# A fifth buffer for the two weight parts, paid with four spare tiles, in a one-core decoder of four layers

## The chip, the core and the metric

The kernel runs on one core of a Trainium2 chip. The metric is the device time in microseconds (us) of one execution, as the median of several runs. The engines are TensorE (PE in the profile; PEld is its weight loading), VectorE (DVE), ScalarE (ACT), GpSimd (POOL) and SyncE (SP, whose queue issues most DMAs).

## The reference

A sequence of 1024 tokens of width 1024, all in float32, passes through a retention layer, a latent-attention (MLA) layer, a gated linear attention layer (GLA) and a feed-forward block. Cut to one layer, and to the form that the others share:

```python
h = rmsnorm(x, g_pre)
proj = h @ w_in                      # 1024 x 1024 @ 1024 x 6144 in the first layer
q, k, v, gate = jnp.split(proj, [...], axis=-1)
...                                  # rope, scores in chunks, running state, group norm
y = (jax.nn.silu(gate) * o) @ w_out
return x + rmsnorm(y, g_post)
```

The last block is two large GEMMs, the first feed-forward GEMM with its activation and the second one back to width 1024.

## The kernel before

**Products.** A float32 operand is split into a high part, cast to the fp32r type, and a low part, the rest: x = hi + lo, w = wh + wl. Each GEMM is three fp32r matmuls that sum in one accumulator: hi with wh (L230), lo with wh (L231), hi with wl (L232), in `mm3`. In `turned_product` (L524 to L526) the activations are the stationary operand and the weights the moving one; a product of 512 columns then comes as two halves of 256. Large GEMMs are made block by block with seven products in place of eight, so weights are needed in sums as well: the raw parts `ws` and `wsc` are loaded, `wsb` and further sums are made on GpSimd (`w_op`, L641).

**Weight parts.** `w_split` makes them from a raw tile: ScalarE copies to `wh` (L632), then VectorE subtracts to get `wl` (L633). `load_parts` does the same for plain weights (L143, L144). All pairs of the kernel come from two rings, `wh` and `wl`, of [128, 1024] tiles (4 KB in a partition), given out in turn. A pair can be written once PE has read the one that stood in its place.

**Jobs and stages.** Stage A (to 510 us) makes the inputs of the retention layer: jobs for q and k, V jobs (turned, seven pairs each) and gate jobs, four of each kind. From 510 to 800 come the retention itself and its output GEMM, then the input of stage B (800 to 1010, with `load_parts`), the attention and its output (to 1390). Stage C (1390 to 1740) makes the inputs of the GLA layer. Into its jobs a side chain is woven, `c_side` and `c_levels`: for each of 8 passes SyncE loads a log-decay `b`, ScalarE makes `qe` and `kd` of it, VectorE multiplies `kd` and `z`, and PE turns `kd` (L1786) and multiplies the levels (`ps_lv`, L1766). The GLA layer's cores and its output follow, to 1960. The first feed-forward GEMM runs to 2234, the second to the end.

**Tiles of the second feed-forward GEMM.** Its operands live in a list of free [128, 512] tiles (2 KB in a partition), `Slots`: `get` takes the first that is free, `put` appends. It works in groups, `FF2_GROUPS = (3, 3, 3, 3, 2, 2)`: a group of three loads `lo<-u` (21 tiles, each split at once into a high and a low part, so 42 tiles) and holds 28 tiles of sums. `F_SLOTS` adds spare tiles to the list:

```python
slots.add(fslots, [f"f{i}" for i in range(F_SLOTS)])
```

**Order.** Each engine works off its own queue in order, and the queues are written when the program is built: a scheduler with a timeline of its own places an instruction once its operands and buffers are free there, weights with high priority. Loads go through SyncE's queue (L122; weights L689). Stores go through ScalarE's queue (L119) in the stages A and B and through SyncE's after that. The number of buffers therefore decides not only how early a pair may be written on the chip, but where each split, load and store stands in its queue.

Of the kernel before, what the change touches and what calls it, by code (L numbers as in the profile page):

```python
# [14 lines left out]
F32R = mybir.dt.float32r  # L15
# [7 lines left out]
P = 128  # L23
# [15 lines left out]
C_WIDE = 2  # L39
C_WAIT = 16  # L40
C_LAST = 3
F_SLOTS = 7
C_TAIL = "01 11 21- 02 A 12 22- w0 w1 A 06 B 07 A 05 B w0 w2 04 A 03 B 16 17 B w1 15 14 13 w2 26- 27- 25- a 24- a 23- b"
C_NORM = "NP"
C_DVE = 3
# [36 lines left out]
def tile_kernel(ctx, tc, a, out):  # L82
# [3 lines left out]
    def pool(stack, name, bufs=1, space=None, side=None):  # L86
        kw = {}
        if space is not None:
            kw["space"] = space
        if side is not None:  # L90
            kw["side"] = side
        return stack.enter_context(
            tc.tile_pool(name=name, bufs=bufs, reuse_waits="tile", **kw)
        )

    cp = pool(ctx, "const")
    wp = pool(ctx, "weights")
# [26 lines left out]
    def load_w(*args, **kw):  # L124
        with tc.high_priority():
            return load_parts(*args, **kw)

    def load_parts(src, scale=None, nk=None):

        c = src.shape[-1]  # L130
        ws = wp.tile([P, 1024], F32, tag="ws", name="ws", bufs=2)[:, :c]
        nc.sync.dma_start(out=ws, in_=src)
        if scale is not None:
            w3 = ws.rearrange("p (k f) -> p k f", k=nk)
            nc.gpsimd.tensor_tensor(
                out=w3,
                in0=w3,
                in1=scale.unsqueeze(2).to_broadcast([P, nk, c // nk]),
                op=ALU.mult,
            )  # L140
        wh = wp.tile([P, 1024], F32R, tag="wh", name="wh", bufs=4)[:, :c]
        wl = wp.tile([P, 1024], F32R, tag="wl", name="wl", bufs=4)[:, :c]
        nc.scalar.activation(out=wh, in_=ws, func=AF.Copy)  # L143
        nc.vector.tensor_tensor(out=wl, in0=ws, in1=wh.bitcast(F32), op=ALU.subtract)  # L144
        return wh, wl
# [9 lines left out]
    def stage(name):  # L155
        return sp.tile([P, HALF], F32, tag="stage", name=name, bufs=4)
# [469 lines left out]
            self.direct(ps, (0, 1))  # L626

    def w_pair():
        return [wp.tile([P, 1024], F32R, tag=t, name=t, bufs=4) for t in ("wh", "wl")]

    def w_split(hi, lo, raw, lo_eng=nc.vector):
        nc.scalar.activation(out=hi, in_=raw, func=AF.Copy)  # L632
# [2 lines left out]
    def w_parts(raw, lo_eng=nc.vector):  # L635
        hi, lo = (t[:, : raw.shape[-1]] for t in w_pair())
        w_split(hi, lo, raw, lo_eng)
        return hi, lo
# [4 lines left out]
    def load_w7(src, pl):  # L643

        q = lambda t, i, n=1: t[:, i * 256 : (i + n) * 256]
        with tc.high_priority():
            ra = wp.tile([P, 1024], F32, tag="ws", name="ws", bufs=2)
            rb = pl.tile([P, HALF], F32, tag="ws7", name="ws7", bufs=1)
            nc.sync.dma_start(out=ra, in_=src)
            b12, b11, b21, b22 = (q(ra, i) for i in range(4))  # L650
            ha, hb = w_pair(), w_pair()

            def into(pair, c, n, src):
                w_split(*(q(t, c, n) for t in pair), src)

            into(ha, 0, 2, q(ra, 0, 2))
            w_op(q(rb, 0), b21, b22, ALU.add)
            w_op(q(rb, 1), b11, q(rb, 0), ALU.subtract)
            into(hb, 0, 2, rb)
            w_op(b21, b21, b11, ALU.subtract)  # L660
            into(ha, 2, 2, q(ra, 2, 2))
            w_op(b12, b12, q(rb, 1), ALU.add)
            into(hb, 2, 1, b12)
        w = {n: (q(ha[0], i), q(ha[1], i)) for i, n in enumerate((2, 1, 7, 4))}
        w.update({n: (q(hb[0], i), q(hb[1], i)) for i, n in enumerate((5, 6, 3))})
        return w

    class W7:
# [10 lines left out]
        def pair(self):  # L679
            return [t[:, : 2 * self.c] for t in w_pair()]  # L680
# [114 lines left out]
    with ExitStack() as ph:  # L795
# [87 lines left out]
        def job_of(n, early=False):  # L883
            product, src, f, i = jobs[n]
            w = W7(src, ap, 2 if product is turned_product else 1)
            if early:
                w.first()
            get = early_get if early else slots.get
            p = on_bank(product, bank5) if early else product
            return w, Fresh(p, get, lambda m, h, ts: f(i, m, h, ts))  # L890
# [17 lines left out]
        for n in range(len(jobs)):  # L908
            last = n == len(jobs) - 1
            drop = x7.drop if last else None  # L910
            if begun:
                w, c = begun.pop(0)
                c.product = jobs[n][0]
                w.rest(n >= 2)
            else:
                w, c = job_of(n)
# [652 lines left out]
    t = stage("mask")[:, : 7 * 64]  # L1569
# [296 lines left out]
    def job_of_c(n, early=False, bank=bank5):  # L1866
        product, src, f, i = c_jobs[n]
        w = W7(src, w7p, 2 if product is turned_product else 1)
        if early:
            w.first()  # L1870
        get = early_get_c if early and n < C_BEGIN else slots.get
        done = lambda m, h, ts: f(i, m, h, ts)
        return w, Fresh(on_bank(product, bank), get, done)
# [23 lines left out]
    for n in range(C_WIDE, len(c_jobs) - C_LAST):  # L1897
        if begun:
            w, c = begun.pop(0)
            w.rest(eng=nc.vector if n < C_DVE else nc.gpsimd)  # L1900
        else:
            w, c = job_of_c(n)
# [130 lines left out]
    for step in C_TAIL.split():  # L2033
# [4 lines left out]
        else:  # L2038
            w, c = last[int(step[0])]
# [51 lines left out]
    fslots = pool(ctx, "f_slots")  # L2091
    slots.add(fslots, [f"f{i}" for i in range(F_SLOTS)])

# [35 lines left out]
    def ff1_job(i, early=False):  # L2129
        w = W7(a["w_ff1"][i], w7p)  # L2130
        if early:
            w.first()
        done = lambda m, h, ts: u_done(i, m, h, ts)
        return w, Fresh(plain_product, slots.get, done)
# [4 lines left out]
    for i in range(16):  # L2139
        drop = x7.drop if i == 15 else None  # L2140
        if begun:
            w, c = begun.pop(0)
            w.rest()
        else:
            w, c = ff1_job(i)
# [283 lines left out]
```

## Time and profile before

| what | before |
| --- | --- |
| runs, us | 2575.43, 2577.38, 2582.12; median 2577.38 |
| profiled execution, us | 2580.32 |
| its span, first to last instruction, us | 2578.5 |
| granted clock of PE, mean | 0.977 |
| busy of the span: PE, DVE, ACT, POOL | 95%, 77%, 44%, 44% |

All rows below are of the profiled execution. Its time holds 1.8 us outside the span, and it lies 2.9 us above the median of the runs. A granted clock of 1.00 is the full 2.4 GHz, the level below it half of that. Names in the rows leave buffer numbers out (`wl` is any tile of that ring); [1.07 <-DVE wl L633] behind a row means that its engine was idle so long before it, and what ended that.

### The profile page before, as it was taken

The numbers are of one execution on the slowest core, as the hardware profiler recorded it, in microseconds if no ns is written. First come the engines' busy times: TensorE is split into PE (matmuls) and PEld (weight loads), VectorE is DVE, ScalarE is ACT, GpSimd is POOL, SyncE is SP. The second block draws the span as 40 slices with busy tenths as digits, with TensorE's granted clock in tenths as the row PEclk, the third lists the DMA queues.
The fourth block names the chain that finished last, engine by engine and source line by source line (L and its number), as shares of the span: only waits on it lengthen the run. The fifth ranks groups of instructions, "written<-read, shape, count | busy, mean of one in ns | idle before, by whom it ended". The sixth has DMA issues, their size and how long they took to land. (4 is left out here: it accounts for less than half of the span.)

```text
span 2578.5 us, 35600 instructions
## 1 busy us (share of the span) xinstructions
PE 2457.3 (95%) x12676; PEld 2058.8 (80%) x12676; DVE 1978.9 (77%) x2948; ACT 1130.4 (44%) x2033; POOL 1122.5 (44%) x834
## 2 busy tenths in 40 slices
PE   7999999999998999999999999989999999999998
PEld 5888888878776788888888788877777888788877
DVE  8787786789998863777659867787888777867886
ACT  7323323254443333555545365564453333543334
POOL 4354453534754521322203244444546666433355
PEclk8999999999998999999999999999999999999999
DMA  6423323533342222122234233456424444644432
GB/s 229 159 86 116 109 78 119 199 116 126 108 137 80 90 99 75 55 63 77 83 121 151 92 127 112 151 172 208 139 90 156 150 151 151 236 141 138 143 131 90
DMA packets 152670, 326.05 MB, mean 126 GB/s; under 512 B 17419, under 2 KB 20875, under 8 KB 152492
## 3 DMA queue, kind: packets, MB, share of 16 engines
q1 hardware_dynamic: 130604, 283.92, 33.4%
q10 hardware_dynamic: 21888, 39.86, 4.1%
q8 instruction: 100, 1.64, 0.3%
q14 instruction: 78, 0.64, 0.1%
HBM read 222.52 MB, written 99.09 MB: 125 GB/s over the span
## 5 line engine op out<-in xcount | busy, mean ns | idle before, releaser
L633 DVE TENSOR_TENSOR wl<-ws,wh 128x1024 fp32r<-128x1024 f32 (+3 forms) x200 | 211.2, 1063 | 24.7 <-ACT wh L632 23.7
L632 ACT ACTIVATE wh<-ws 128x1024 fp32r<-128x1024 f32 (+3 forms) x200 | 142.7, 725 | 198.3 <-PE ps L231 104.2
L641 POOL TENSOR_TENSOR wsb<-wsc 128x512 f32<-128x512 f32 (+2 forms) x72 | 101.4, 1409 | 252.7 <-issue 168.9
L230 PE MATMUL ps<-hi,wh 128*128 128x512 f32 (+1 forms) x488 | 185.8, 381 | 2.2 <-DVE y L2188 1.4
L232 PE MATMUL ps<-hi,wl 128*128 128x512 f32 (+1 forms) x488 | 183.9, 381 | 3.5 <-DVE wl L633 2.6
L231 PE MATMUL ps<-lo,wh 128*128 128x512 f32 (+1 forms) x488 | 185.4, 380 | 0.0
L632 ACT ACTIVATE wh<-wsb 128x1024 fp32r<-128x1024 f32 (+2 forms) x76 | 73.6, 968 | 222.6 <-PE ps L231 162.7
L641 POOL TENSOR_TENSOR ws<-ws,wsb 128x512 f32<-128x512 f32 (+2 forms) x72 | 102.1, 1418 | 122.2 <-DVE wl L633 104.7
L1430 POOL TENSOR_SCALAR p<-p,rl 128x512 f32<-128x512 f32 (+2 forms) x96 | 61.8, 655 | 191.7 <-DVE rl L1428 96.6
L641 POOL TENSOR_TENSOR wsb<-ws,wsb 128x512 f32<-128x512 f32 (+2 forms) x72 | 115.6, 1606 | 64.3 <-DMA ws<-w_a 41.1
L553 DVE TENSOR_TENSOR y<-ps,y 128x512 f32<-128x512 f32 x112 | 76.8, 686 | 72.2 <-PE ps L232 45.1
L553 DVE TENSOR_TENSOR y<-ps,one 128x512 f32<-128x512 f32 x108 | 73.7, 686 | 71.6 <-PE ps L232 27.8
L553 DVE TENSOR_TENSOR one<-ps,one 128x512 f32<-128x512 f32 x168 | 114.1, 682 | 12.7 <-PE ps L232 11.6
L633 DVE TENSOR_TENSOR wl<-wsc,wh 128x1024 fp32r<-128x1024 f32 (+2 forms) x76 | 109.5, 1445 | 8.6 <-ACT wh L632 8.1
L633 DVE TENSOR_TENSOR wl<-wsb,wh 128x1024 fp32r<-128x1024 f32 (+2 forms) x76 | 98.7, 1299 | 18.4 <-ACT wh L632 17.8
L232 PEld LDWEIGHTS ps<-hi,wl 128*128 128x128 f32 x488 | 91.7, 188 | 25.0 <-DVE wl L633 4.5
L641 POOL TENSOR_TENSOR wsc<-wsc,ws 128x512 f32<-128x512 f32 (+2 forms) x72 | 110.7, 1538 | 0.0
L230 PEld LDWEIGHTS ps<-hi,wh 128*128 128x128 f32 x488 | 91.7, 188 | 22.3 <-DVE y L2188 1.8
L231 PEld LDWEIGHTS ps<-lo,wh 128*128 128x128 f32 x488 | 91.7, 188 | 18.8
L2188 DVE TENSOR_TENSOR y<-ps,y 128x512 f32<-128x512 f32 x124 | 83.4, 683 | 29.6 <-PE ps L232 29.2
L632 ACT ACTIVATE wh<-wsc 128x1024 fp32r<-128x1024 f32 (+2 forms) x76 | 73.2, 969 | 59.3 <-PE ps L231 39.3
L188 DVE TENSOR_TENSOR lo<-lo,hi 128x512 fp32r<-128x512 f32 x106 | 77.5, 762 | 26.0 <-ACT hi L187 24.0
(468 smaller groups left out, 8543.5 us busy)
## 6 DMA issues: line engine op xcount, KB each, us to landing
lo<-u SPq DMA_DIRECT2D x98, 256.0 KB, 5.2
ws<-w_ff SPq DMA_DIRECT2D x23, 512.0 KB, 3.9
ws<-w_a SPq DMA_DIRECT2D x21, 512.0 KB, 4.7
u<-y SPq DMA_DIRECT2D x42, 256.0 KB, 2.1
ws<-w_b SPq DMA_DIRECT2D x17, 512.0 KB, 3.5
wsc<-w_a SPq DMA_DIRECT2D x16, 512.0 KB, 4.5
v<-v SPq DMA_DIRECT2D x32, 256.0 KB, 3.3
gate<-g SPq DMA_DIRECT2D x32, 256.0 KB, 3.4
```

The source lines that it names most:

```text
L188: (lo_eng or nc.vector).tensor_tensor(out=lo, in0=src, in1=hi.bitcast(F32), op=ALU.subtract)
L230: nc.tensor.matmul(ps, lh, rh, start=start, stop=False)
L231: nc.tensor.matmul(ps, lh, rl, start=False, stop=False)
L232: nc.tensor.matmul(ps, ll, rh, start=False, stop=stop)
L553: nc.vector.tensor_tensor(out=o, in0=p, in1=i, op=ALU.add)
L632: nc.scalar.activation(out=hi, in_=raw, func=AF.Copy)
L633: lo_eng.tensor_tensor(out=lo, in0=raw, in1=hi.bitcast(F32), op=ALU.subtract)
L641: eng.tensor_tensor(out=o, in0=x, in1=y, op=op)
L1430: nc.gpsimd.tensor_scalar(out=pr, in0=pr, scalar1=rl, scalar2=0.0, op0=ALU.mult, op1=ALU.add)
L2188: nc.vector.tensor_tensor(out=t, in0=ps, in1=t, op=ALU.add)
```

## The change

Both rings of weight parts get a fifth tile (8 KB more in each partition together), in `load_parts` and `w_pair`. The list of tiles of the second feed-forward GEMM gets three spare tiles, where it had seven (8 KB less). One line more at the top moves all lines below by one: L633 of before is L634 after.

```diff
-F_SLOTS = 7
+F_SLOTS = 3
+W_BUFS = 5
...
-        wh = wp.tile([P, 1024], F32R, tag="wh", name="wh", bufs=4)[:, :c]
-        wl = wp.tile([P, 1024], F32R, tag="wl", name="wl", bufs=4)[:, :c]
+        wh = wp.tile([P, 1024], F32R, tag="wh", name="wh", bufs=W_BUFS)[:, :c]
+        wl = wp.tile([P, 1024], F32R, tag="wl", name="wl", bufs=W_BUFS)[:, :c]
...
     def w_pair():
-        return [wp.tile([P, 1024], F32R, tag=t, name=t, bufs=4) for t in ("wh", "wl")]
+        return [wp.tile([P, 1024], F32R, tag=t, name=t, bufs=W_BUFS) for t in ("wh", "wl")]
```

Each engine issues the same instructions as before, in another order. Three places show how.

ScalarE's queue in the first V job of stage A, around 155 to 185 us; `wh_1398` and `wh_1402` are the first two pairs of the job, `wh_1424` the fifth, and L119 or L120 are stores of q and k. Before:

```order
L632 ACTIVATE wh_1398<-ws_1390 128x1024
L119 DMA k_0_1_0_1211<-y_1161 128x512
L119 DMA q_0_0_1_1232<-one_1104 128x512
L119 DMA q_1_0_0_1294<-y_1287 128x512
L632 ACTIVATE wh_1402<-ws_1394 128x1024
L632 ACTIVATE wh_1411<-wsb_1406 128x1024
L119 DMA k_1_1_1_1346<-y_1338 128x512
L632 ACTIVATE wh_1420<-wsb_1415 128x1024
...
L865 ACTIVATE y_1542<-y_1542,r4_389 128x256 x2
L632 ACTIVATE wh_1424<-wsc_1392 128x1024
```
After:

```order
L633 ACTIVATE wh_1398<-ws_1390 128x1024
L120 DMA k_0_1_1_1190<-y_1176 128x512
L560 ACTIVATE one_1272<-ps_7_1259 128x512
L633 ACTIVATE wh_1402<-ws_1394 128x1024
L120 DMA k_0_1_0_1211<-y_1161 128x512
L120 DMA q_0_0_1_1232<-one_1104 128x512
L120 DMA q_1_0_0_1294<-y_1287 128x512
L633 ACTIVATE wh_1411<-wsb_1406 128x1024
L120 DMA k_1_1_1_1346<-y_1338 128x512
L633 ACTIVATE wh_1420<-wsb_1415 128x1024
L633 ACTIVATE wh_1424<-wsc_1392 128x1024
L560 ACTIVATE one_1488<-ps_7_1438 128x512
```
`wh_1402` has gone ahead of three stores, and `wh_1424` ahead of the two evictions `one` and of the scaling of `y_1542`. On VectorE, whose queue is not shown, `wl_1403` stands seven instructions earlier than before and `wl_1425` four, `wl_1421` where it stood.

PE's queue in stage C, where the side chain's transposes of `kd` stand among the products `ps_7` of a job around 1585 us. Before:

```order
L524 MATMUL ps_7_15497<-wh_15352,x2h1_13082 128x256
L525 MATMUL ps_7_15497<-wl_15353,x2h1_13082 128x256
L1786 MATMUL ps_kd_14962<-ident_75,kd_14952 128x128 x4
L1753 MATMUL ps_qk_14970<-q_14942,k_14943 128x128 x4
L526 MATMUL ps_7_15497<-wh_15352,x2l1_13083 128x256
```
After:

```order
L525 MATMUL ps_7_15550<-wh_15352,x2h1_13082 128x256
L526 MATMUL ps_7_15550<-wl_15353,x2h1_13082 128x256
L1787 MATMUL ps_kd_14962<-ident_75,kd_14952 128x128 x4
L1754 MATMUL ps_qk_14970<-q_14942,k_14943 128x128 x4
L527 MATMUL ps_7_15550<-wh_15352,x2l1_13083 128x256
```
The chain's two operations have moved out of the product `ps_7_15497` into the one behind it, `ps_7_15550`; 24 matmuls of 256 columns that stood behind them now stand ahead. The chain's matmuls stand 20 to 24 rows later all through 1500 to 1650 us, 14 at 1658 us, 8 at 1678 us, and where they were at 1688 us. VectorE's operations of the chain stand two to five rows later.

SyncE's queue at the end of the loads of a group of the second feed-forward GEMM, around 2298 us; `lo_21489` is the last tile of this group, `lo_21902` and `lo_21907` are tiles of the next. Before:

```order
L122 DMA lo_21474<-u4_5_19296 128x512
L122 DMA lo_21479<-u3_3_18986 128x512
L122 DMA lo_21484<-u3_4_19142 128x512
L122 DMA lo_21489<-u3_5_19298 128x512
L122 DMA lo_21902<-u1_6_19444 128x512
L122 DMA lo_21907<-u1_7_19600 128x512
L689 DMA wsc_21700<-w_ff2_1 128x768
L689 DMA ws_21698<-w_ff2_1 128x768
```
After:

```order
L690 DMA wsc_21700<-w_ff2_1 128x768
L123 DMA lo_21474<-u4_5_19296 128x512
L123 DMA lo_21479<-u3_3_18986 128x512
L123 DMA lo_21484<-u3_4_19142 128x512
L123 DMA lo_21489<-u3_5_19298 128x512
L690 DMA ws_21698<-w_ff2_1 128x768
L690 DMA wsc_21802<-w_ff2_1 128x768
```
The two loads of the next group are gone from here (they stand among the next group's own loads), and a weight load has come between the last tiles.

## Rows read from the trace of the kernel before

**Rows 1.** The page: the span, then busy time, share and instructions of each engine.

```profile
span 2578.5 us, 35600 instructions
PE 2457.3 (95%) x12676; PEld 2058.8 (80%) x12676; DVE 1978.9 (77%) x2948; ACT 1130.4 (44%) x2033; POOL 1122.5 (44%) x834
```

**Rows 2.** Waits of PE, all: waiting group, releaser, us in total, times, longest.

```profile
PE ps L525 <- DVE wl L633: 12.2, 16, 1.1
PE ps_lv L1766 <- DVE z L1744: 10.5, 6, 3.1
PE ps_kd L1786 <- DVE kd L1711: 9.3, 4, 4.0
...
PE ps L232 <- DVE wl L633: 6.4, 4, 3.8
...
PE ps_grp L232 <- DVE wl L144: 4.1, 1, 4.1
```

**Rows 3.** Windows: busy us (instructions) of each engine, PE's clock, DMA share, GB/s.

```profile
115.00:510.00 395.00, 382.76 (x2273) 335.80 (x2272) 302.44 (x322) 114.66 (x169) 190.74 (x109) 1.00 0.34 114
```

**Rows 4.** Timeline of PE in the first V job: start, us, operation, idle before it.

```profile
166.09 0.38 PE L525 MATMUL ps<-wl,x1h 128*128 128x256 f32 x1 [1.07 <-DVE wl L633]
166.32 0.28 PE L526 MATMUL ps<-wh,x1l 128*128 128x256 f32 x1
...
166.67 0.28 PE L526 MATMUL ps<-wh,x1l 128*128 128x256 f32 x1
...
177.97 0.38 PE L525 MATMUL ps<-wl,x6h 128*128 128x256 f32 x1 [0.95 <-DVE wl L633]
...
184.38 0.38 PE L525 MATMUL ps<-wl,x7h 128*128 128x256 f32 x1 [0.87 <-DVE wl L633]
```

**Rows 5.** Timeline of ACT in the first V job.

```profile
161.87 1.06 ACT L632 ACTIVATE wh<-ws 128x1024 fp32r<-128x1024 f32 x1 [11.30 <-DVE y L850]
...
181.20 0.91 ACT L865 ACTIVATE y<-y,r 128x256 f32<-128x256 f32 x2 [7.42 <-DVE y L553]
182.02 1.05 ACT L632 ACTIVATE wh<-wsc 128x1024 fp32r<-128x1024 f32 x1
```

**Rows 6.** Timeline of DVE in the first V job.

```profile
175.71 2.21 DVE L633 TENSOR_TENSOR wl<-wsb,wh 128x1024 fp32r<-128x1024 f32 x1
...
183.10 2.36 DVE L633 TENSOR_TENSOR wl<-wsc,wh 128x1024 fp32r<-128x1024 f32 x2 [1.68 <-ACT wh L632]
```

**Rows 7.** Windows: width, then busy us of PE, PEld, DVE, ACT, POOL, PE's clock.

```profile
125.00:160.00 35.00, 35.00 (x152) 28.20 (x151) 30.12 (x33) 7.21 (x9) 20.03 (x12) 1.00 0.32 106
160.00:170.00 10.00, 8.93 (x61) 8.06 (x60) 9.80 (x11) 2.01 (x2) 4.76 (x3) 1.00 0.09 36
170.00:180.00 10.00, 9.05 (x77) 8.84 (x77) 9.88 (x8) 2.03 (x3) 8.99 (x6) 1.00 0.05 18
180.00:187.00 7.00, 5.91 (x45) 5.30 (x45) 4.98 (x7) 3.61 (x6) 0.00 (x0) 1.00 0.52 165
```

**Rows 8.** Windows, stage C.

```profile
1390.00:1740.00 350.00, 322.54 (x1991) 282.42 (x1990) 269.51 (x430) 189.73 (x379) 138.20 (x97) 0.92 0.39 129
```

**Rows 9.** Timeline of PE in stage C, at two waits for the side chain.

```profile
1584.59 1.09 PE L1786 MATMUL ps_kd<-ident,kd 128*128 128x128 f32 x4 [3.96 <-DVE kd L1711]
...
1688.87 2.36 PE L1766 MATMUL ps_lv<-z 128*120 128x64 f32 x13 [2.02 <-DVE z L1744]
```

**Rows 10.** Timeline of SP in stage C: start, us from first to last issue, DMA.

```profile
1565.45 10.95 SPq L119 DMA_DIRECT2D cq<-y  x2
1576.50 0.37 SPq L122 DMA_DIRECT2D b<-cb  x1
```

**Rows 11.** Timeline of SP at the first group boundary of the second feed-forward GEMM.

```profile
2284.88 13.90 SPq L122 DMA_DIRECT2D lo<-u  x20
```

**Rows 12.** Timeline of DVE in that group.

```profile
2309.22 0.68 DVE L188 TENSOR_TENSOR lo<-lo,hi 128x512 fp32r<-128x512 f32 x1
```

**Rows 13.** Windows, the group from 2285 to 2340.

```profile
2285.00:2340.00 55.00, 55.00 (x238) 44.35 (x237) 43.02 (x59) 24.23 (x40) 17.51 (x14) 1.00 0.46 150
```

**Rows 14.** Waits of PE from 2234 to the end.

```profile
PE ps L232 <- DVE wl L633: 2.6, 3, 1.7
...
PE ps L232 <- DVE wl L144: 1.0, 2, 0.6
```

## The prediction

> **What bounds the kernel now.** The summary of engines comes first: TensorE (PE) is busy 2457.3 of 2578.5 us, 95% [rows 1]. Anything that a fifth buffer can give has to come out of the 121 us in which PE stands idle, so the list of PE's waits comes next. Weight parts are the releaser in only some of it: 12.2 us at L525 in 16 waits, 6.4 us at L232, and 4.1 us at the grouped product's `wl` [rows 2]. Other work releases the rest: 10.5 us wait for `z` and 9.3 us for `kd`, the side chain of stage C. So at most some 23 us, 0.9% of the time, hangs on the ring at all.
>
> The 16 waits of L525 are four in each of the four V jobs of stage A, whose products are turned; they are all the idle time that PE has from 115 to 510 us, 395 - 382.76 = 12.2 us [rows 3]. In the first of these jobs PE's timeline shows three of the four: 1.07, 0.95 and 0.87 us [rows 4]; 12.2 / 4 is 3.05 us a job. What each waits for is read one engine further back. `wh` on ScalarE starts at 161.87 after 11.30 us of idleness that a store's source, y of L850 on VectorE, ended: it stood behind stores of `k` and `q` in ScalarE's queue. The `wh` of 182.02 stood behind two scalings of y, the first of which waited 7.42 us [rows 5]. On VectorE the splits follow: 2.21 us for the one at 175.71, 2.36 us for the two at 183.10 [rows 6]. The table of windows says why this stretch is tight: VectorE is busy 9.80 and 9.88 of 10 us in 160 to 180, against 30.12 of 35 us before it [rows 7].
>
> **The change part by part.** No instruction is added or taken away; the same 35600 stand in another order, so every term is one of place.
>
> *V jobs.* The two order excerpts of ScalarE show the gain. `wh_1402` goes ahead of the three stores, so its wait for y ends; on VectorE its `wl_1403` stands seven instructions earlier. The first stall, 1.07 us, goes. For the second stall, 0.95 us, `wl_1421` keeps its row; it comes sooner only as far as the splits taken out ahead of it found idle time in 125 to 160, where VectorE has 35 - 30.12 = 4.9 us [rows 7]. I count half, 0.45 us. Of the third, `wh_1424` is now right behind `wh_1420`, but the same product needs `wh_1428` six matmuls (0.7 us at 0.35 us for three [rows 4]) later, and that still stands behind the scaling of y_1542; I count nothing. So 1.5 us a job, 6 us in four jobs. Bounds: nothing, if VectorE merely trades one late operation for another; 12.2 us, if all 16 waits go. I take the middle, because VectorE is full for 20 us but not before.
>
> The price of a moved split depends on its company. With GpSimd idle (0.00 us of 180 to 187 [rows 7]) two splits took 2.36 us, 1.18 us each [rows 6]. With GpSimd busy 8.99 of 10 us one took 2.21 us. A split that moves from idle company to busy company costs 1.03 us more of VectorE.
>
> The Trainium skill, SBUF — State Buffer, section "SBUF: two separate sides", says that VectorE and GpSimd share a port pair as an exclusive lock, which a VectorE operation with two SBUF inputs takes against a GpSimd operation that reads SBUF, and that the loser blocks. That speaks against moving splits into stretches where GpSimd works; the two durations agree in direction, and by the rule the term of the V jobs would be nearer 2 us than 6.
>
> *Stage C* (1390 to 1740). Its windows row has PE at 322.54 of 350 us and the clock at 0.92 [rows 8], but its waits for PE name `kd` and `z`, never a weight part. What changes is where the side chain's matmuls stand among the products: `ps_kd_14962` comes 24 matmuls later, which is 24 x 0.117 = 2.8 us of products that now run before PE comes to it, instead of after. Today PE waits there 3.96 us [rows 9]. If the chain's next pass hangs on the products too, the 2.8 us are kept. It does in part: the load of `b` for this pass left the queue of SyncE at 1576.50, right behind two stores of product outputs that took from 1565.45 to 1576.40 to go [rows 10]. If the chain runs by its own pace, the 2.8 us are given back at 1688.87, where PE waits 2.02 us for `z` [rows 9] and this place does not move. VectorE's operations of the chain stand two to five rows later, behind splits that came forward. Bounds: -5.6 us (2.8 us kept in each of two runs of shifted places) and +17.7 us (one split of 2.21 us ahead of the chain in each of the stage's 8 passes). I take -2 us: VectorE is 77% busy there (269.51 of 350 us [rows 8]), so a split has room in most passes.
>
> *Second feed-forward GEMM.* A group of three block products takes 42 x tiles and 28 sums out of the list of tiles. Four spare tiles fewer mean that at each of four group boundaries two loads of the next group can no longer be made ahead. The SyncE excerpt shows it: `lo_21902` and `lo_21907` leave the end of the burst. Twenty loads go in 13.90 us, 0.70 us each [rows 11], and a split of one takes 0.68 us on VectorE [rows 12]. Two late tiles are thus up to 1.4 us late. PE stands still nowhere in this group (55.00 of 55 us [rows 13]), and VectorE has 55 - 43.02 = 12 us to spare, so most of it is covered. Bounds: nothing, and 4 x 1.4 = 5.6 us if the refill had no slack. I take 1.5 us.
>
> *Last stretch.* From 2234 on PE waits 2.6 us for `wl` of L633 and 1.0 us for that of L144 [rows 14]. In the new order these splits stand two to five rows earlier after 2500; I count 1.4 us, the part of it there (0.42 of the 2.6, and the 1.0). Bounds 0 and 3.6 us.
>
> *Input of stage B.* One wait of 4.1 us [rows 2] is for a split that moves eight rows forward on VectorE. Right behind it PE waits for `xl` and `raw`, which the same engine makes, so what the split gains they lose: nothing, between -4.1 and +2.2 us (one slow split). The start of the kernel keeps its order up to the waits.
>
> **Sum.** -6 - 2 + 1.5 - 1.4 + 0 = -7.9 us. The profiled execution took 2580.32 us in a span of 2578.5, which gives 2572.4 us for one like it. It lies 2.9 us above the median 2577.38, so against the median the forecast is 2569.5 us. 0.3% of the median, about what a measurement of this kernel can tell from no change, is 7.7 us.
>
> **The rivals.**
>
> *The waits only change their names.* VectorE is full in 160 to 180, and the brought-forward splits meet GpSimd, which is busy 20.03 of 35 us in 125 to 160 [rows 7]. If two splits a job become 1.03 us longer, VectorE arrives 2.06 us later at `wl_1421`, which eats the 0.45 us and part of the 1.07: some 0.5 us a job is left, 2 us in all. Stage C gives back its 2.8 us at 1688.87. Then -2 + 0 + 1.5 - 1.4 = -1.9, 2575.5 us. For it: the windows row. Against it: 4.9 us of idle VectorE just ahead. The rule named above would lead here.
>
> *Fewer spare tiles cost what the ring gains.* If the refill at a group boundary has no slack, the term is 5.6 us instead of 1.5: -3.8 in the sum, 2573.6 us. Against it: PE did not wait once in those groups.
>
> *Slower: splits ahead of the side chain.* In stage C, VectorE works off weight splits first and `kd` and `z` afterwards; PE waits for exactly these today, 9.3 and 10.5 us [rows 2], so each delay goes straight on the path when the chain sets the pace. Eight passes at 1.18 to 2.21 us are 9.4 to 17.7 us. In place of the -2 this makes the sum +3.5 to +11.8, 2581 to 2589 us. It decides, by 0.3%, from (7.7 + 5.9) / 8 = 1.7 us a pass on. For it: no wait of this stage is for a weight part, so only the order can act. Against it: the products that come first fill PE meanwhile.
>
> **Chances.** The forecast and better: 0.45. Waits that change their names: 0.28. Spare tiles: 0.10. Slower: 0.17. Faster by over 0.3% thus has 0.45, within 0.3% 0.38, slower 0.17. If the upper bounds of the V jobs (-12.2) and of stage C (-5.6) held with the rest as it stands, the time would be 2559.7; a little under this, 2557, is the lower end. The upper end is 2586, inside the slower rival, which leaves about a tenth on either side. The forecast's own range is 2557 to 2573.
>
> **What would show it.** In the V jobs, the waits L526 <- `wl` of L634 should fall from 12.2 to about 6 us and the one near 166 us should be gone; no fall, with VectorE still full in 160 to 180, is the first rival. In stage C, the waits for `kd` and `z` (19.8 us together) should fall by some 2 us and PE's clock there stay at 0.92; a rise means the slower rival. At the group boundaries, near 2297 and every 55 us on, PE should show no wait over 0.5 us; waits for `lo` or `hi` there would be the spare tiles. The prediction fails if a stage outside these terms, whose order moves too, takes or gives more than 5 us.

## The result and the profile after

The changed kernel takes 2552.48 us (median of 6 runs, 2544.43 to 2555.42) against 2580.68 us before (6 runs): a ratio of 0.9895, with an interval of 0.9881 to 0.9909. By the ratio that is 27 us or 1.05% faster, more than three times the 7.9 us of the forecast, and the time lies below its lower end of 2557.

The summary of engines of the changed kernel, in the form of [rows 1], shows that PE's share rose by one point only, and that VectorE and GpSimd are each some 60 us less busy with the same number of instructions. PE's idle time, span less busy time, fell from 121.2 to 109.9 us. That is 11.3 of the 26.1 us between the two spans; the other 14.8 us are busy time of PE, for the same 12676 matmuls. (The 207 instructions more of the first line are in none of these groups.)

```profile
span 2552.4 us, 35807 instructions
...
PE 2442.5 (96%) x12676; PEld 2051.0 (80%) x12676; DVE 1919.3 (75%) x2948; ACT 1133.6 (44%) x2033; POOL 1062.9 (42%) x834
```

Windows fixed in time can't be compared between kernels that run apart. Both execute the same 12676 matmuls, though, nearly in the same order, so the table below cuts the traces at the same counts: a stage runs from the start of its first matmul to the start of the next stage's first. The cuts are at matmul 0, 420, 2700, 3800, 4950, 7050, 10000, 12250 and 12675 of PE's timeline. Stage C stands together with the cores behind it, since their matmuls mix at the border. "Start" begins with the first matmul, at 8 us.

| stage, us | before | after | difference |
| --- | --- | --- | --- |
| start | 112.7 | 112.1 | -0.5 |
| jobs of stage A | 393.2 | 383.6 | -9.7 |
| retention | 235.0 | 232.2 | -2.8 |
| its output, input of B | 269.1 | 267.2 | -1.9 |
| attention | 368.4 | 371.3 | +2.9 |
| stage C and its cores | 580.3 | 571.3 | -9.0 |
| feed-forward GEMMs | 527.2 | 523.8 | -3.4 |
| end | 76.0 | 74.9 | -1.0 |

Each column is one profile. How far two profiles of one order lie apart shows in the run spares_only below, whose matmuls have the order of before up to 2218 us: its stages up to there lie within 2.4 us of the column before.

**Stage A.** The waits of PE in the V jobs, where [rows 2] had 12.2 us in 16 waits, are now four:

```profile
PE ps L526 <- DVE wl L634: 5.7, 4, 1.7
```

The timeline of PE in the first V job has one wait left of the three of [rows 4]; it is for the low part of the sixth pair, the last of 1024 columns:

```profile
182.29 0.38 PE L526 MATMUL ps<-wl,x7h 128*128 128x256 f32 x1 [1.70 <-DVE wl L634]
```

ScalarE's timeline there shows why it is left. The fifth and sixth high part stood together behind the scaling of y before (182.02 in [rows 5]). The fifth now stands right behind the fourth (167.25), but the sixth (178.83) still stands behind the scaling, which itself waited 8.20 us:

```profile
167.25 1.05 ACT L633 ACTIVATE wh<-wsc 128x1024 fp32r<-128x1024 f32 x1
...
177.47 0.91 ACT L866 ACTIVATE y<-y,r 128x256 f32<-128x256 f32 x2 [8.20 <-DVE y L554]
...
178.83 1.06 ACT L633 ACTIVATE wh<-wsc 128x1024 fp32r<-128x1024 f32 x1 [0.46 <-ACT y L866]
```

A window of the same stretch as in [rows 7] shows VectorE relieved: 8.05 of 10 us busy in 170 to 180, where it had been 9.88.

```profile
170.00:180.00 10.00, 10.00 (x88) 10.00 (x87) 8.05 (x9) 2.08 (x4) 4.04 (x3) 1.00 0.32 102
```

**Stage C.** The waits of PE from 1364 to 1730 answer to the `kd` and `z` of [rows 2]: `kd` fell from 9.3 to 2.2 us, `z` rose from 10.5 to 11.4. Nothing names a weight part, as before.

```profile
PE ps_lv L1767 <- DVE z L1745: 11.4, 6, 4.0
...
PE ps_kd L1787 <- DVE kd L1712: 2.2, 1, 2.2
```

The windows row of the stage, beside [rows 8], has PE's clock at 0.94 instead of 0.92:

```profile
1380.00:1726.00 346.00, 320.58 (x2039) 281.26 (x2038) 281.31 (x446) 191.76 (x384) 133.72 (x102) 0.94 0.40 133
```

**The second feed-forward GEMM** has no wait for L634's `wl` any more, where [rows 14] had 2.6 us; PE does not wait at all in its groups. From 2213 to the end four waits are left, 2.1 us in all, of which one is for a weight part:

```profile
PE ps L233 <- DVE wl L145: 0.5, 1, 0.5
```

So two terms carry most of the gain, the jobs of stage A (expected, though larger) and stage C with its cores (expected at -2 us); the GEMMs' 3.4 us come next. The experiments ask of each whether the fifth buffer itself brought it.

### The profile page after: what moved, and what is told of

It is laid out like the page before. It is cut to its first block, busy times and chain, and to the rows that moved or that the text cites. A ratio compares the mean times of both kernels' runs of the same rounds, so it can differ in the third digit from the quotient of the medians.

```text
span 2552.4 us, 35807 instructions
## 1 busy us (share of the span) xinstructions
PE 2442.5 (96%) x12676; PEld 2051.0 (80%) x12676; DVE 1919.3 (75%) x2948; ACT 1133.6 (44%) x2033; POOL 1062.9 (42%) x834
## 4 chain that ended last, share of the span: by engine, by line
PE 69%; DVE 18%; issue 4%; ACT 3%; DMA 3%; POOL 2%; SPq 0%; ACTq 0%; DVEq 0%; POOLq 0%
PE ps L233 14%; PE ps L232 14%; PE ps L231 14%; DVE wl L634 3%; PE ps L526 2%; PE ps L525 2%; PE ps L527 2%; PE ps_g L232 1%; PE ps_g L233 1%; PE ps_g L231 1%; PE ps_lv L1767 1%; PE pt L1456 1%; DVE z L1745 1%; PE ps_out L231 1%; PE ps_out L232 1%
## 5 line engine op out<-in xcount | busy, mean ns | idle before, releaser
L633 ACT ACTIVATE wh<-ws 128x1024 fp32r<-128x1024 f32 (+2 forms) x200 | 142.9, 725 | 137.0 <-PE ps L232 102.8
L634 DVE TENSOR_TENSOR wl<-ws,wh 128x1024 fp32r<-128x1024 f32 (+2 forms) x200 | 187.6, 946 | 17.8 <-ACT wh L633 17.1
L232 PE MATMUL ps<-lo,wh 128*128 128x512 f32 (+1 forms) x488 | 185.8, 381 | 0.0
L642 POOL TENSOR_TENSOR wsb<-wsc 128x512 f32<-128x512 f32 (+2 forms) x72 | 94.2, 1308 | 176.0 <-issue 94.1
L633 ACT ACTIVATE wh<-wsc 128x1024 fp32r<-128x1024 f32 (+2 forms) x76 | 73.4, 968 | 175.1 <-PE ps L232 173.3
L633 ACT ACTIVATE wh<-wsb 128x1024 fp32r<-128x1024 f32 (+2 forms) x76 | 73.6, 968 | 144.3 <-PE ps L232 73.5
L642 POOL TENSOR_TENSOR wsb<-ws,wsb 128x512 f32<-128x512 f32 (+2 forms) x72 | 96.3, 1337 | 64.0 <-DMA ws<-w_c 30.4
L634 DVE TENSOR_TENSOR wl<-wsc,wh 128x1024 fp32r<-128x1024 f32 (+2 forms) x76 | 103.7, 1366 | 20.0 <-ACT wh L633 19.5
L232 PEld LDWEIGHTS ps<-lo,wh 128*128 128x128 f32 x488 | 92.3, 189 | 19.1
L642 POOL TENSOR_TENSOR wsc<-wsc,ws 128x512 f32<-128x512 f32 (+2 forms) x72 | 102.0, 1416 | 0.0
L634 DVE TENSOR_TENSOR wl<-wsb,wh 128x1024 fp32r<-128x1024 f32 (+2 forms) x76 | 88.7, 1167 | 3.6 <-ACT wh L633 3.2
L189 DVE TENSOR_TENSOR lo<-lo,hi 128x512 fp32r<-128x512 f32 x106 | 81.8, 804 | 12.2 <-ACT hi L188 12.2
```

What stands on the lines that cost most here:

```text
L189: (lo_eng or nc.vector).tensor_tensor(out=lo, in0=src, in1=hi.bitcast(F32), op=ALU.subtract)
L232: nc.tensor.matmul(ps, lh, rl, start=False, stop=False)
L634: lo_eng.tensor_tensor(out=lo, in0=raw, in1=hi.bitcast(F32), op=ALU.subtract)
L642: eng.tensor_tensor(out=o, in0=x, in1=y, op=op)
```

## The experiments

Ratios are against the kernel before, with 95% intervals. Stage times are cut at the matmul counts above.

**Spare tiles alone.** The kernel before with one line of the change:

```diff
-F_SLOTS = 7
+F_SLOTS = 3
```

> Rings of four as before, three spare tiles instead of seven; only the second feed-forward GEMM is ordered differently. Theory (the spare tiles are covered): within 2 us of before, PE without a wait in the groups. Rival (the 3.4 us that the changed kernel won at the start of the second feed-forward GEMM come from the new order of the loads there, not from the ring): 3 us faster than before. The forecast's term: 1.5 us slower, at most 5.6.

Measured: 2576.66 us, ratio 0.9991 (0.9980 to 1.0002). The feed-forward GEMMs took 523.9 us, against 523.8 in the changed kernel, and the end took 78.1, 2.1 more than before. The rival had it for the GEMMs: the 3.4 us are the spare tiles'. (The total, 2 us faster with an interval from 5 us faster to 0.5 slower, decides nothing.) With fewer free tiles, SyncE loads the first weights of the second GEMM (`wsc_20943`, `ws_20941`) ahead of the first tile `lo_20836`, where before they stood behind two such loads, and the waits for `wl` at its start are gone. At the end, waits of PE from 2485 on in this run, the smaller list costs 1.3 us more for the last plain weights than the 1.0 of [rows 14]:

```profile
PE ps L232 <- DVE wl L144: 2.3, 2, 1.7
```

**Five pairs in one half of the program only.** The rings stand in a memory pool of their own that is closed at 800 us and opened anew with another size (seven spare tiles with five pairs up to 800 us, three with five behind):

```diff
+W_BUFS = (5, 4)                      # ring5_from_800: (4, 5)
...
-    lslots = pool(ctx2 := ctx.enter_context(ExitStack()), "a_slots")
+    wr = [pool(ctx2 := ctx.enter_context(ExitStack()), "ring_a"), W_BUFS[0]]; lslots = pool(ctx2, "a_slots")
...
-    ctx2.close()
+    ctx2.close(); wr[:] = pool(ctx, "ring"), W_BUFS[1]
```

> A ring of five pairs up to 800 us and of four behind it, seven spare tiles. Theory (each stage keeps what its own ring wins): 12 us faster than before, 9.7 of it in the jobs of stage A and 2.8 in the retention behind them, nothing from 800 on. Rival (stages behind give it back, as a lead on PE ends in the next wait for a chain): less than 6 us faster.

> A ring of four pairs up to 800 us and of five behind it, three spare tiles. Theory: 13 us faster than before, with some 15 us won in stage C, 6 lost in the cores behind it and 4 won in the second feed-forward GEMM; the first 800 us as before. Rival (stage C's gain came from the state in which stage A left the engines): under 6 us faster.

Measured: 2555.55 us, 0.9910 (0.9893 to 0.9927), with five pairs up to 800 us; 2579.16, 0.9999 (0.9987 to 1.0011), with five behind. The closing has a price of its own: the input of stage B took 281.1 and 286.7 us instead of 269.1, with PE idle for 25 and 32 us there. That spoils the totals, not the stages; the first run is 23 us faster even so, where the theory had said 12. The jobs of stage A took 381.0 us with five pairs and 391.7 with four, so that term belongs to the ring. Stage C and its cores took 572.7 us with five pairs, but 564.8 with four. The theory that each stage keeps what its own ring wins had no explanation for that.

**The side chain later, by hand.** Theory then: the chain stood later among the products, and the ring only brought that about.

```diff
         while not side.free:
             yield 1
+        yield 1
```

> The kernel before, rings of four, with the side chain of stage C put one bank of a product (24 matmuls) later in the program. Theory (the order of the chain against the products is what stage C won by, the buffer only brought it about): 8 to 15 us faster than before, the waits for kd shorter. Rival (the weights being ready earlier is what counts): within 3 us of before, since the ring is as it was; or slower, if the chain sets the pace.

Measured: 2579.99 us, 1.0006 (0.9994 to 1.0018), and 579.3 us for stage C and its cores. This run tells little: in the program that came out, the chain's `kd` matmuls stood where they had stood before, and only some earlier ones had moved, forward. The scheduler undid the edit, so the theory was not put to its test.

**Two sizes without a hand-over.** The pairs come from single tiles by a counter whose turn changes from one size to another; spare tiles three in all four:

```diff
+    ring_n, turn_w = [W_BUFS[0]], {"wh": -1, "wl": -1}
+    def w_tile(t): turn_w[t] = (turn_w[t] + 1) % ring_n[0]; return wp.tile([P, 1024], F32R, tag=f"{t}{turn_w[t]}", name=t, bufs=1)
...
-    ctx2.close()
+    ctx2.close(); ring_n[0] = W_BUFS[1]
```

> The base of the four: pairs given out by a counter over tiles of their own, four up to 800 us and four behind it, three spare tiles. All theories: within 5 us of before.

> Five pairs up to 800 us, four behind it, with no hand-over of memory between the two. Theory (what stage C wins comes with the order that the program gets behind a stage A of five, not from C's own ring): 20 us or more faster than two_rings_44, some 12 of it before 750 us and the rest in stage C. Rival (each stage wins by its own ring): 12 us faster, stage C as in two_rings_44.

> Four pairs up to 800 us, five behind it. Theory: under 5 us faster than two_rings_44, since stage A stays as it is. Rival (each stage wins by its own ring): 10 us or more faster, in stage C.

> Five pairs throughout by the same counter. Both theories: 20 to 28 us faster than two_rings_44. If it is slower than two_rings_54, a ring of five behind 800 us has a price of its own.

| run | ratio | jobs of A | C and cores | end |
| --- | --- | --- | --- | --- |
| two_rings_44 | 0.9943 (0.9927 to 0.9960) | 393.0 | 572.3 | 78.6 |
| two_rings_54 | 0.9920 (0.9905 to 0.9936) | 386.8 | 570.6 | 77.8 |
| two_rings_45 | 0.9964 (0.9950 to 0.9978) | 393.2 | 579.6 | 73.4 |
| two_rings_55 | 0.9936 (0.9917 to 0.9955) | 386.9 | 580.8 | 74.9 |

Stage A follows its ring again, by 6 us here and not by 10; the clock has the rest (see the next experiment). Stage C follows something else: both kernels with five pairs behind 800 us are 7 to 10 us slower there than both with four, the reverse of what the changed kernel seemed to show, and with four pairs throughout it is already 8 us faster than before. The base, expected within 5 us of before, was 13 us faster, and both theories on the totals missed. Five pairs throughout were 4 us slower than five up to 800 us alone. The two intervals overlap, so this only hints at a price of the later ring; one place of it is shown further below.

Two runs with the same later ring also have the same order on every engine in stage C: two_rings_44 and two_rings_54 throughout, two_rings_45 and two_rings_55 up to 1800 us. Each pair agrees within 1.7 us there, while the two pairs lie 7 to 10 us apart.

The end follows the later ring. With three spare tiles it takes 77.8 to 78.6 us with four pairs and 73.4 to 75.3 with five, over all nine such kernels; before, with four pairs and seven spare tiles, it took 76.0. The fifth pair wins some 3.5 us there and the spare tiles lose 2. Five pairs with seven spare tiles were not run.

**One ring only, and more of it.** In `load_parts` and `w_pair` each ring gets its own number:

```diff
-W_BUFS = 5
+W_BUFS = dict(wh=5, wl=4)            # wh4_wl5: 4, 5;  wh6_wl4: 6, 4
-F_SLOTS = 3
+F_SLOTS = 5                          # wh6_wl4: 3
```

> Five buffers for the high parts alone, four for the low ones, five spare tiles. Theory (the ring of high parts is the one that holds the splits back, since the copy comes first): the jobs of stage A take 6 to 10 us less than before, the waits of L526 there fall from 12.2 to under 8 us, as with both rings at five. Rival (a pair is only as early as its later half): 16 waits and 12 us as before. Stage C goes its own way in either case; its order here is another one again.

> Five buffers for the low parts alone, five spare tiles. The order of every engine is that of before up to stage C. Theory: the jobs of stage A as before, 393 us and 12 us of waits, although the low parts have one buffer more. Rival (a buffer more lets the chip run ahead even in an unchanged order): fewer than 12 us of waits. In all within 5 us of before.

> Six buffers for the high parts, four for the low ones, three spare tiles, the memory of the changed kernel. The last high part of each V job now stands ahead of the scaling of y. Theory: the one wait of 1.6 us that is left in each V job of the changed kernel goes too, and the jobs of stage A take 380 us or less. Rival (the low part's own ring of four, or VectorE, holds it): 383 us or more, as in the changed kernel.

Measured: 0.9963 (0.9950 to 0.9976), 1.0022 (1.0012 to 1.0033) and 0.9967 (0.9955 to 0.9980). The low ring alone leaves the V jobs as they were, 12.2 us in 16 waits, as expected; the whole is 6 us slower, most of it in stage C (584.1 us), in another order again. The high ring alone was expected to do what both do, and made the jobs of stage A slower: 396.6 us with five high parts and 395.2 with six, against 393.2 before. PE's timeline of the first V job with five high and four low parts shows what happened:

```profile
178.73 0.58 PE L526 MATMUL ps<-wl,x6h 128*128 128x256 f32 x1 [2.81 <-DVE wl L634]
```

The waits of a job have joined into one of 2.8 us, for the low part of the fourth pair. Up to here the ring of low parts is all that differs from the changed kernel. The sum of the waits is no worse than before (11.4 us against 12.2), but behind each of the four the granted clock falls to its lower level (with six high parts, behind three of four). Windows of this kernel and of the changed one, in this order, with PE's clock in the third place from the end:

```profile
115.00:505.00 390.00, 378.63 (x2202) 334.26 (x2201) 299.76 (x318) 112.00 (x162) 182.53 (x108) 0.98 0.33 110
...
176.00:186.00 10.00, 7.27 (x50) 7.27 (x51) 9.16 (x9) 4.68 (x9) 4.07 (x3) 0.83 0.39 136
```

```profile
115.00:505.00 390.00, 384.13 (x2316) 339.88 (x2315) 290.53 (x332) 119.19 (x180) 181.80 (x118) 1.00 0.36 120
```

A clock of 0.98 over 390 us is some 8 us lost. The changed kernel has one wait a job too, of 1.6 to 1.7 us in three of them and 0.9 in the fourth, and keeps 1.00. Both rings are needed, then: a pair is as early as its later half.

It does not take one long wait to lower the clock. In two_rings_54 the waits of the four jobs sum to 5.5 us, less than in the changed kernel, but in three of the jobs two of them stand only one matmul apart:

```profile
181.05 0.38 PE L525 MATMUL ps<-wh,x7h 128*128 128x256 f32 x1 [0.66 <-ACT wh L633]
182.31 0.39 PE L526 MATMUL ps<-wl,x7h 128*128 128x256 f32 x1 [0.88 <-DVE wl L634]
```

Behind two of these three the clock fell, to 0.84 in the window from 176 to 186 us, and over 115 to 505 us it was 0.99. That is where the stage's 386.8 us differ from the 383.6 of the changed kernel; two_rings_55 has the same picture. What exactly decides whether the clock falls, no run here settles.

**The stores out of ScalarE's queue.** The kernel before, with

```diff
-QS = lambda nc: (nc.scalar, nc.sync)
+QS = lambda nc: (nc.sync, nc.sync)
```

> The kernel before, rings of four, with the stores of the stages A and B issued by SyncE instead of ScalarE. Theory (the buffer, not the stores ahead in ScalarE's queue, held the first high part back): 12 us of waits in the V jobs as before. Rival (a blocked queue was the cause): the first wait of each V job goes, 1.07 us by its row and 0.28 us beside it, some 5 us in all.

Measured: 2578.88 us, 0.9999 (0.9990 to 1.0008), jobs of stage A 392.9 us, 16 waits and 12.3 us. The waits stayed, as the theory had it, but not for its reason. The second high part of the first V job, which started at 161.87 behind the stores [rows 5], now started at 157.77, when PE freed its buffer. Its low part started at 164.75, against 164.81 before:

```profile
157.77 1.06 ACT L632 ACTIVATE wh<-ws 128x1024 fp32r<-128x1024 f32 x1 [7.32 <-PE ps L231]
```

```profile
164.75 1.23 DVE L633 TENSOR_TENSOR wl<-ws,wh 128x1024 fp32r<-128x1024 f32 x1
```

So the stores did hold the high part back, by 4.1 us, and it cost PE nothing: the wait of 1.07 us hangs on the place of the low part in VectorE's queue, which is the same in both kernels. In the changed kernel this split stands seven instructions earlier and starts at 154.40.

**Stage C in another order, rings held fixed.** A count that sets how early the rows of stage C's input are taken up; all that stands ahead of stage C keeps its order.

```diff
-C_WAIT = 16
+C_WAIT = 15                          # or 17
```

> The kernel before with a wait count of 15 for 16 ahead of stage C, which only gives stage C another order. Theory (order, not the buffer): stage C and its cores, 580 us before, move by 5 us or more in at least one of the two runs with rings of four, and all stages ahead stay within 3 us. Rival (the buffer): both stay within 3 us of 580.

> The kernel before with a wait count of 17 for 16 ahead of stage C. Theory and rival as with a count of 15: 5 us or more away from 580 us in one of the two, or both within 3 us.

> The changed kernel with a wait count of 15 for 16. Theory: stage C and its cores, 571 us in the changed kernel, move by 5 us or more in at least one of the two runs with rings of five, up or down. Rival: both stay within 3 us of 571. The jobs of stage A keep 384 us in all cases.

> The changed kernel with a wait count of 17 for 16. Theory and rival as with a count of 15: 5 us or more away from 571 us in one of the two, or both within 3 us.

| run | ratio | C and cores | jobs of A |
| --- | --- | --- | --- |
| order_15_ring4 | 0.9977 (0.9965 to 0.9989) | 572.2 | 393.3 |
| order_17_ring4 | 0.9984 (0.9974 to 0.9995) | 573.9 | 393.2 |
| order_15_ring5 | 0.9909 (0.9893 to 0.9925) | 572.3 | 383.2 |
| order_17_ring5 | 0.9895 (0.9880 to 0.9910) | 570.8 | 381.9 |

With rings of four, these profiles show 6 and 8 us of the 9 that the changed kernel won here; by the ratios the two kernels are 6 (count 15) and 4 us (count 17) faster than before. The 6 us of count 17 are not safe: from 1440 us on every engine of that kernel has the order of stores_on_sp, and there stage C and its cores took 578.0 us. One order thus differs by up to 4 us between profiles, and the 8 us of count 15 stand clear of that. With rings of five, neither moved by 5 us, which the theory had wanted of one. Both kernels with five run as fast as the changed one, within the intervals; no run beats it clearly.

## Why the prediction was wrong

By the stage table the terms compare so, forecast first: jobs of stage A -6 and -9.7; stage C with its cores -2 and -9.0; the GEMMs, where the spare tiles were to act, +1.5 and -3.4; the end -1.4 and -1.0; all stages without a term 0 and -2.3.

**The premise.** "Anything that a fifth buffer can give has to come out of the 121 us in which PE stands idle" is the first step that failed. Of the 26.1 us between the spans 11.3 came out of idle time. The rest is busy time, and two parts of it can be named: the time at the lower level of the clock fell from 117.5 to 103.5 us, worth at most 7 us at half speed, and a wait costs PE more than its idle time, as the V jobs show. The list behind "at most some 23 us" is also off in itself. It leaves out a group for high parts, and counts 3.8 us of L232 that belong, like this group, to the first 115 us:

```profile
PE ps L230 <- ACT wh L632: 6.3, 2, 4.4
```

**The V jobs: the mechanism was right, the size was not.** The first two waits of a job went and the third stayed behind the scaling of y_1542. The waits fell to 5.7 us, the "about 6" of the text, but by two errors that cancel: the second wait (0.95 us) went whole and not by half, and the third grew, from 0.87 and 0.16 us to 1.70 in the first job. The reading that ScalarE's stores caused the first wait was wrong (stores_on_sp); the split's place on VectorE did. The step of the sum that failed is "1.5 us a job, 6 us in four jobs": the stage won 9.7. A wait of PE costs more than its row. In [rows 4] the matmul of 166.09 is preceded by this one:

```profile
164.74 0.28 PE L525 MATMUL ps<-wl,x1h 128*128 128x256 f32 x1
```

There are 1.35 us between these two starts, and 0.23 to the next start, where 0.117 each is the rule. That is 1.35 + 0.23 - 2 x 0.117 = 1.35 us lost for a row that says 1.07, so 0.28 us beside the row. Before, PE stood idle 17 times in these jobs (one short time for a high part), 12.2 us in all, and after 5 times, 5.9 us: 12 x 0.28 + (12.2 - 5.9) = 9.7, the whole difference. The same sum fits the other kernels: four waits and 4.3 us in ring5_to_800 give 393.2 - 7.9 - 13 x 0.28 = 381.7, measured 381.0; with five high parts alone, 393.2 - 0.8 - 13 x 0.28 + 8 for the clock is 396.8, measured 396.6. The upper bound of 12.2 us for this term was too low for the same reason.

**Splits that meet GpSimd.** The first rival charged two splits a job with 1.03 us more each. That price was paid. The fifth and sixth pair's splits took 2.36 us together before; in the first V job of the changed kernel they are

```profile
173.31 2.32 DVE L634 TENSOR_TENSOR wl<-wsc,wh 128x1024 fp32r<-128x1024 f32 x1
...
179.93 2.31 DVE L634 TENSOR_TENSOR wl<-wsc,wh 128x1024 fp32r<-128x1024 f32 x1 [1.90 <-ACT wh L633]
```

and the next two jobs are like it. The sixth ends at 182.24, and the wait that is left ends at 182.29. In the fourth job the sixth split met no GpSimd operation and took 1.23 us, and the wait is 0.88 us in place of 1.6 to 1.7. The rival's time did not come all the same: the splits stand earlier by more than this, and the fourth one fell from 2.21 to 1.23 us.

Nor is it true that busy company alone makes a split dear: the one of 157.20 before took 1.22 us, with GpSimd busy for 1.17 of them. There the GpSimd operation started 0.05 us after the split and took 2.34 us; those beside the two dear splits had started before them, at 172.21 and 179.87. The Trainium skill (SBUF — State Buffer, "SBUF: two separate sides") says of the shared port pair that the operation that starts first holds it for the whole instruction, while the other blocks. These three meetings agree with it. The prediction took from the page that the dearer splits would cost most of the gain, and they did not.

In sum the changed kernel lets the two engines meet less often: both are busy at once for 801 us, where it was 939. The mean of the plain split fell from 1063 to 946 ns; this is its row after, which belongs to the page's costliest groups:

```profile
L634 DVE TENSOR_TENSOR wl<-ws,wh 128x1024 fp32r<-128x1024 f32 (+2 forms) x200 | 187.6, 946 | 17.8 <-ACT wh L633 17.1
```

VectorE's busy time follows the rings: 1979 to 1984 us in the seven kernels with four pairs throughout, 1960 and 1964 with five up to 800 us, 1930 in both with five behind it, 1916 to 1919 with five throughout.

**Stage C: the other term that failed** is "Bounds: -5.6 us [...] and +17.7 us", and the reasoning behind it that prices places one by one from the order. Its sign was right and its size was -9.0 instead of -2. It was also put to the wrong account. The waits for `kd` and `z` did fall, from 19.8 to 13.6 us, but others came, and PE's idle time in the stage with its cores did not fall: 40.6 us before, 41.8 after. What fell is the time at the lower level of the clock, from 68 to 58 us, worth at most 5 us; the forecast wanted the clock to stay.

Does the order do this, or the ring? With four pairs there, stage C and its cores took 564.8 to 580.3 us over nine kernels; with five, 570.8 to 580.8 over six. Two profiles of one order lie up to 4 us apart. At rings of four and with all earlier stages held in order, the count of 15 won 8 us, by 58 us at the lower clock and 38.7 us idle; two_rings_44 also won 8 us, by idle time (33.7 us) with the clock as before. That another order moves this stage at a fixed ring is therefore shown. That the 9 us of the changed kernel are the order's alone is argued from it and not shown, and which feature of an order shortens idle time or raises the clock stays open.

One place does hang on the ring. Behind the cores, where PE needs `r` for a norm, GpSimd makes three weight sums first in the changed kernel, although the input of `r` is there at 1916.2; before, `r` stood ahead of them. This is the last of the sums, then `r`, and PE's wait:

```profile
1919.43 1.71 POOL L642 TENSOR_TENSOR wsc<-wsc,ws 128x512 f32<-128x512 f32 x1
1921.11 1.46 POOL L313 TENSOR_TENSOR r<-var,neghalf 128x4 f32<-128x4 f32 x1
```

```profile
1922.62 1.65 PE L321 MATMUL ps_rb<-ident,r 128*128 128x128 f32 x6 [4.72 <-POOL r L313]
```

All six kernels with five pairs there have this wait, 4.7 us each; in the others it is 0.9 us at most. So the fifth pair let weight work overtake something that PE needs sooner, and the changed kernel won its 9 us in spite of it.

**Spare tiles: wrong sign.** "I take 1.5 us" for refills that come late; no boundary cost anything, and the start of the GEMM won 3.4 us because weights went ahead of tiles. The end lost 2.1 us. In sum the spare tiles are worth -1 us, by spares_only within 0.2% of before.

**Last stretch.** The 1.4 us were meant for the ring, which won some 3.5 us at the end, as the kernels with three spare tiles show; the part at the start of the GEMM was the spare tiles'.

**The rest.** Input of B: nothing forecast, -1.9 measured. Retention and attention were not named: -2.8 and +2.9. Kernels with four pairs took 229.7 to 235.0 us in the retention, so its gain can't be told from the spread between profiles; in the attention they took 367.2 to 369.0 and most with five 369.7 to 371.3, so some 2 us are likely a price of the ring. The slower rival, splits ahead of the side chain, did not come: VectorE was at 281.31 of 346 us in the stage, and PE's idle time in the two windows of stage C itself was 25.4 us after 27.5.

## What to carry to other kernels

Where a scheduler writes the queues, a buffer more is a change of order everywhere: cost the stage that the buffer serves from its waits, and give every other stage a spread. Neutral edits (a count that only reorders) measure it; profile one order twice as well, since here the same order came out up to 4 us apart. Don't price a short wait of PE by its row alone; take the distance of the starts on both sides. Look behind the gains for what the earlier work overtook: here a norm's `r` on GpSimd, for 4.7 us. And lift two halves of one operand together: with one ring longer than the other, four short waits became one long one, and the clock made it dearer than before.

## What the runs showed that was not expected

- Four waits of 0.2 to 1.1 us in a V job left the granted clock at 1.00, and so did one of 1.7 us; one of 2.8 us took it to 0.83 in the 10 us around it, and so did, in two of three jobs, waits of 0.66 and 0.88 us with one matmul between them (0.84).
- A wait of PE for the low part of a turned product cost some 0.28 us beside its row, in every job before and after.
- The same number of VectorE and GpSimd instructions took 60 us less on each of the two engines with five pairs throughout, and VectorE 15 to 50 us less with five in one half of the program only.
- A split beside GpSimd took 1.2 or 2.3 us by which of the two operations had started first, 0.05 us apart in one case and 0.06 in another.
